# Transposed products with the activations' high and low parts side by side

## The chip, the cores and the metric

One NeuronCore of one Trainium2 chip runs the whole program. The metric is the device time of one execution in microseconds (us); lower is better. The engines are TensorE (PE in the profile, its loads of a stationary operand PEld), VectorE (DVE), ScalarE (ACT), GpSimd (POOL) and SyncE (SP), which issues the DMAs.

## The reference

One decoder block over 256 positions of width 1024, all in float32:

```python
h = rms_norm(x, norm1_g)
proj = h @ w_in                                  # [q | k | v | z | xBC | dt | gate_attn | gate_ssd]
y_attn = moba_attention(rms_norm(q), rms_norm(k), v) @ w_attn_o        # 16 heads of 64
y_ssd = ssd_mixer(z, xbc, dt_raw, ...) @ w_ssd_o                       # 2048 -> 1024
mixed = sigmoid(g_attn) * y_attn + sigmoid(g_ssd) * y_ssd
x = x + mixed @ w_out
x = x + peer_ffn(rms_norm(x, norm2_g), w_peer_q, keys1, keys2, u_tab, v_tab)

def peer_ffn(xn, w_q, keys1, keys2, u_tab, v_tab):
    q = (xt @ w_q).reshape(T, 8, 256)            # 8 heads
    s1 = einsum('thd,hkd->thk', q[..., :128], keys1)    # 128 keys each
    s2 = einsum('thd,hkd->thk', q[..., 128:], keys2)
    v1, i1 = top_k(s1, 16); v2, i2 = top_k(s2, 16)
    sv, pos = top_k(all sums v1 + v2, 16)        # 16 of 16384 experts for each head and token
    gw = softmax(sv)
    act = einsum('td,thkd->thk', xt, u_tab[eidx])
    return einsum('thk,thkd->td', gelu(act) * gw, v_tab[eidx])
```

## The kernel before

A product in float32 precision is made of three matmuls in TensorE's fp32r type. Each operand is held as a high part (the value rounded to fp32r) and a low part (the rest), and high by high, high by low and low by high are summed in PSUM. Weights come from HBM as 392 tiles of 128x1024 (512 KB), in one fixed order: the blocks of w_in, then w_attn_o and w_ssd_o, w_out, w_peer_q, the 128 tiles of u_tab, the 128 of v_tab. For each tile, `ahead` issues the load into a ring of three raw buffers, the copy on ScalarE that makes the high part (`wh`, line 128) and the subtraction that makes the low part (`wl`, on VectorE in line 138, on GpSimd in line 133 for one tile in three or four); `wh` and `wl` are rings of four. In this text the subtraction is called the split. `next_w` hands out the next tile and lets this pipeline run three tiles ahead.

The work goes through the weights in that order.

- The blocks of w_in: for each of 8 groups, products for q and k, v, z, and the two inputs of the convolution. The steps of attention, convolution and scan are generators in the list `active`; `tick()`, called twice in every product of 8 chunks, advances each by one step, so that their work falls between the matmuls. The last 8 blocks are the gates (line 695): 128 columns of each gate to a block.
- The output projections (line 705): for each of four blocks of 256 columns, `pA` (attention, 8 chunks) and `pS` (scan, 16 chunks), mixed with the gates into `mh` and `ml`.
- w_out with the residual, the second norm, and the transposed activations `xh`, `xl`.
- The queries, one product for each of 8 heads, with `head_scores` behind it. Here the top-16 searches and the one-hot selections begin (`picks`, paced so that each step is queued on VectorE behind the latest split).
- u_tab, 64 pairs of tiles (`u_pair`): every token against every expert, then Gelu into `gA`. When the picks are done (`start` is the pair at which that happens), the gate matrices follow, built from one-hots eight tokens at a time between the remaining pairs, and multiplied into `gA`.
- v_tab, 64 pairs of tiles, summed in four PSUM banks over all experts.

A *transposed* product (`product_T`, and the loop of `u_pair`) has the weights as the stationary operand and the activations as the moving one, 256 columns (the tokens) wide; its output has 128 weight columns on the partitions and the tokens along the free axis. Two such column tiles share a PSUM buffer of 512 columns. Three PSUM buffers (tag "mm") take turns for all products. A chunk is 128 rows of the summed dimension:

```python
mm(ps[:, ct], h[:, c], xh[:, k], start=k == 0, stop=False)
mm(ps[:, ct], h[:, c], xl[:, k], start=False, stop=False)
mm(ps[:, ct], lo[:, c], xh[:, k], start=False, stop=k == 8 * n - 1)
```

The order of instructions on each engine is made by the framework's scheduler from the order of the program, the dependencies and a few explicit ones (`issue_after`).

Of the kernel before, what the change touches and what calls it, by code (L numbers as in the profile page):

```python
# [9 lines left out]
F32 = mybir.dt.float32  # L10
F32R = mybir.dt.float32r
# [50 lines left out]
def tile_hybrid_block(ctx: ExitStack, tc: tile.TileContext, x, n1g, wblk, wdt, qkg, cw, cb, dtb,  # L62
# [11 lines left out]
    neghalf = const.tile([128, 16], F32, name="neghalf")  # L74
    V.memset(neghalf, -0.5)
    xt = const.tile([128, 2, D], F32, name="xt")
    hTh = const.tile([128, 8, T], F32R, name="hTh", tag="nh")
    hTl = const.tile([128, 8, T], F32R, name="hTl", tag="nl")

    def K(ins):  # L80

# [8 lines left out]
    def f32(ap):  # L90
        return ap.bitcast(F32)
# [50 lines left out]
    def next_w():  # L142
        i = state["next"]
        ahead()
        state["next"] += 1
        h, lo = parts.pop(i)
        return h, lo
# [3 lines left out]
    def tick():  # L151

        for it in list(active):
            if next(it, "end") == "end":
                active.remove(it)
# [9 lines left out]
    def product_T(ps, n, xh, xl):  # L165

        for ct in range(2):
            for f in range(n):
                h, lo = next_w()
                h = h.rearrange("p (c n) -> p c n", c=8)  # L170
                lo = lo.rearrange("p (c n) -> p c n", c=8)
                for c in range(8):
                    k = 8 * f + c
# [3 lines that stand above are left out]
                    if c % 4 == 3:  # L177
                        tick()

    def natural_w():  # L180
        w = []
        for f in range(2):
            h, lo = next_w()
            w += [(h[:, 256 * c:256 * c + 256], lo[:, 256 * c:256 * c + 256]) for c in range(4)]
        return w

    def product_half(ps, tt, w, xh, xl, late=False):
        s = slice(128 * tt, 128 * tt + 128)
        for f in range(2):
            terms = [(k, i) for k in range(4 * f, 4 * f + 4) for i in range(3)]  # L190
            if late:
                terms.sort(key=lambda t: (0, 2, 1)[t[1]])
            for n, (k, i) in enumerate(terms):
                lhs, rhs = ((xh, w[k][0]), (xh, w[k][1]), (xl, w[k][0]))[i]
                mm(ps[:, tt], lhs[:, k, s], rhs, start=f == n == 0, stop=f == 1 and n == 11)  # L195
            tick()

    def product_N(ps, xh, xl, late=False):

        w = natural_w()  # L200
        for tt in range(2):
            product_half(ps, tt, w, xh, xl, late)

    def rstd_of(pool, ss, n, inv, name):
        r = pool.tile([128, n], F32, name=name + "m", tag=f"rm{n}", bufs=2)
# [8 lines left out]
    def ps_tile(tag, name):  # L214
        return psum.tile([128, 512], F32, name=name, tag=tag, bufs={"mm": 3, "tr": 2, "at": 3}[tag])

    with tc.tile_pool(name="pa", bufs=1) as pa, ExitStack() as ctx2:
# [101 lines left out]
        dist = pa.tile([128, 384], F32, name="dist")  # L319
        mask = pa.tile([128, 384], F32, name="mask")  # L320

        attnh = pa.tile([128, 8, T], F32R, name="attnh")
        attnl = pa.tile([128, 8, T], F32R, name="attnl")
        yh = pa.tile([128, 16, T], F32R, name="yh")
        yl = pa.tile([128, 16, T], F32R, name="yl")


        dth = pa.tile([128, 2, 32], F32, name="dth")
# [8 lines left out]

        def w384(name):
            return wk.tile([128, 384], F32, name=name, tag="w384", bufs=W384)

        def half(t):
            return t.rearrange("p (a n) -> p a n", a=2)

        def decay():
            wdh = wk.tile([128, 8, 32], F32R, name="wdh", bufs=1)
# [320 lines left out]
            vsb[b] = v  # L666
            yield

        def take_gate(g, ps):
            A.activation(tg[:, :, g], ps, AF.Tanh, scale=0.5)  # L670
            yield

        active.append(decay())
# [17 lines left out]
            product_N(half(ps), hTh, hTl)  # L691
            active.append(zgate(g, ps))
        for g in range(NG):
            ps = half(ps_tile("mm", f"psg{g}"))
            product_T(ps, 1, hTh, hTl)
            active.append(take_gate(g, ps))
        while active:
            tick()

# [3 lines left out]
        mh = pm.tile([128, 8, T], F32R, name="mh", bufs=1)  # L703
        ml = pm.tile([128, 8, T], F32R, name="ml", bufs=1)
        for b in range(4):
            pA = ps_tile("mm", "pA").rearrange("p (c t) -> p c t", c=2)
            product_T(pA, 1, attnh, attnl)
            pS = ps_tile("mm", "pS").rearrange("p (c t) -> p c t", c=2)
            product_T(pS, 2, yh, yl)
            m1 = pm.tile([128, 2, T], F32, name="m1", tag="w512", bufs=W512)  # L710
            V.scalar_tensor_tensor(m1, tg[:, 0, 2 * b:2 * b + 2], 1.0, pA, op0=OP.add, op1=OP.mult)
            m2 = pm.tile([128, 2, T], F32, name="m2", tag="w512", bufs=W512)
            V.scalar_tensor_tensor(m2, tg[:, 1, 2 * b:2 * b + 2], 1.0, pS, op0=OP.add, op1=OP.mult)
            V.tensor_tensor(m1, m1, m2, op=OP.add)
            A.activation(mh[:, 2 * b:2 * b + 2], m1, AF.Copy, scale=0.5)
            V.scalar_tensor_tensor(ml[:, 2 * b:2 * b + 2], m1, 0.5, f32(mh[:, 2 * b:2 * b + 2]),
                                   op0=OP.mult, op1=OP.subtract)
        ss4 = pm.tile([128, 2, 4], F32, name="ss4", bufs=1)
        ss2 = pm.tile([128, 2], F32, name="ss2", bufs=1)
        xh = const.tile([128, 8, T], F32R, name="xh", tag="nh")  # L720
        xl = const.tile([128, 8, T], F32R, name="xl", tag="nl")

        def residual(b, tt, po):
            s = slice(256 * b, 256 * b + 256)
# [67 lines left out]
    def head_scores(h, ps):  # L792
        qT = tk.tile([128, 2, T], F32, name="pqT", tag="pqT")
        if h == 0:
            q = tk.tile([128, 2, T], F32, name="pq", tag="pqT")
            A.activation(q, ps, AF.Copy)
            yield
            ps = ps_tile("tr", "pqt").rearrange("p (c t) -> p c t", c=2)
            for f in range(2):
                for tt in range(2):  # L800
                    nc.tensor.transpose(ps[:, f, 128 * tt:128 * tt + 128], q[:, tt, 128 * f:128 * f + 128], ident)
            yield
        A.activation(qT, ps, AF.Copy)
        yield
        yield
        p2 = ps_tile("tr", "pss").rearrange("p (a n) -> p a n", a=4)
        for tt in range(2):
            for f in range(2):
                mm(p2[:, 2 * tt + f], qT[:, f, 128 * tt:128 * tt + 128], ks[:, f, h], start=True, stop=True)
        yield  # L810
        s = tk.tile([128, 4, 128], F32, name="sco", tag="sco", bufs=8)
        A.activation(s, p2, AF.Copy)
        scores[h] = s
# [103 lines left out]
    def halves(a, b):  # L917

        r = []
        for i in range(2):  # L920
            lo, hi = max(a, 64 * i), min(b, 64 * i + 64)
            if lo < hi:
                r.append((lo, hi, gA[i][:, lo - 64 * i:hi - 64 * i]))
        return r

    def u_pair(jp):
        ps = ps_tile("mm", "psu").rearrange("p (j t) -> p j t", j=2)
        for jj in range(2):
            h, lo = next_w()
            h = h.rearrange("p (c n) -> p c n", c=8)  # L930
            lo = lo.rearrange("p (c n) -> p c n", c=8)
            for c in range(8):
                mm(ps[:, jj], h[:, c], xh[:, c], start=c == 0, stop=False)  # L933
                mm(ps[:, jj], h[:, c], xl[:, c], start=False, stop=False)  # L934
                mm(ps[:, jj], lo[:, c], xh[:, c], start=False, stop=c == 7)  # L935
                if c % 4 == 3:
                    tick()
        td = done["t"]
        (_, _, dst), = halves(2 * jp, 2 * jp + 2)
        if td < T:  # L940
            A.activation(dst[:, :, td:], ps[:, :, td:], AF.Gelu)
        if td > 0:
            gt = pb.tile([128, 2, T], F32, name="gel", tag="gel", bufs=2)
            A.activation(gt[:, :, :td], ps[:, :, :td], AF.Gelu)
            V.tensor_tensor(dst[:, :, :td], dst[:, :, :td], gt[:, :, :td], op=OP.mult)
# [34 lines left out]
    active.append(picks)  # L980
    active.insert(0, head_scores(0, psq0))
    for h in range(1, 8):
        ps = ps_tile("mm", "psq").rearrange("p (c t) -> p c t", c=2)
        product_T(ps, 1, xh, xl)
        active.insert(0, head_scores(h, ps))
    start = None
    for jp in range(64):
        u_pair(jp)
        if start is None and (done["picks"] == 2 or jp >= 30):
            while done["picks"] < 2:  # L990
                tick()
            tkctx.close()
            pb2 = ctx.enter_context(tc.tile_pool(name="pb2", bufs=1))
            gA[1] = pb2.tile([128, 64, T], F32, name="gA1")
            start = jp
            one_hots(0)
        elif start is not None:
            n = 62 - start
            k = jp - start - 1
            if k < n:  # L1000
                for q in range(32 * k // n, 32 * (k + 1) // n):
                    gate_group(q, 2 * jp + 2)
                    if q + 1 < 32:
                        one_hots(q + 1)
# [96 lines left out]
```

## Time and profile before

| | |
|---|---|
| median of 3 runs | 1246.58 us (1246.37 to 1247.64) |
| the profiled execution | 1246.86 us, of it 1244.8 us in the span of the profile |
| TensorE busy | 1228.4 us, 9005 matmuls |
| VectorE busy | 897.4 us |
| ScalarE busy | 633.9 us |
| GpSimd busy | 296.0 us |
| granted TensorE clock, mean | 0.997 of full |
| gates / output projections / queries | 282 to 342 / 342 to 411 / 444 to 491 us |
| u_tab before the gate matrices, with them / v_tab | 491 to 654, 654 to 892 / 892 to 1244 us |

Matmuls are pipelined: one is shown as busy from its start to its modelled end, and the next one starts before that, so the pace of a stretch is read from start to start. In a view of windows the columns are the stretch, its length, the busy time of PE, PEld, DVE, ACT and POOL with the count of instructions, the granted clock, the DMA share and GB/s. In a timeline they are start and duration in us, engine, line, operation, what is written and read, and in brackets how long the engine had stood idle before and what it waited for. In a group of instructions, the busy time in us and the mean of one in ns stand behind the bar.

### The profile page before, as it was taken

Reading aid. Unit: us, or ns where it says so; the run is one execution under the profiler, and the core shown is the slowest. Engines: PE = TensorE matmul, PEld = TensorE weight load, DVE = VectorE, ACT = ScalarE, POOL = GpSimd, SP = SyncE. Lnnn points to the kernel's source line nnn. Section 1 sums busy time; section 2 is a strip of 40 time slices with the busy share of each in tenths; the row PEclk is TensorE's granted clock in tenths of the full one; section 3 lists DMA queues with packets and bytes.
Section 4 is the critical chain, followed back from the end, with each engine's and each line's share of the span. In section 5 each row is a group of like instructions: output and inputs, shape, how many; then the busy total and the mean of one; then the engine's idle time right before and its main releaser. Section 6 shows DMA issues by size and latency. Waiting matters only on the chain.

```text
span 1244.8 us, 22716 instructions
## 1 busy us (share of the span) xinstructions
PE 1228.4 (99%) x9005; PEld 1140.7 (92%) x9005; DVE 897.4 (72%) x1583; ACT 633.9 (51%) x975; POOL 296.0 (24%) x160
## 2 busy tenths in 40 slices
PE   8999999999999999999999999999999999999998
PEld 6989989999999999999999999999988888888887
DVE  6888989899334566688697888999855555555554
ACT  5666666666434454554544544444445454444442
POOL 3355354444222122232323222222100000000000
PEclk8999999999999999999999999999999999999999
DMA  5434444444455464546555455444455555555553
GB/s 193 173 136 154 169 156 166 153 145 143 171 202 186 137 220 153 185 155 209 180 172 168 153 170 160 157 168 158 165 195 194 195 188 201 188 194 194 196 193 118
DMA packets 60345, 215.15 MB, mean 173 GB/s; under 512 B 7600, under 2 KB 8144, under 8 KB 60112
## 3 DMA queue, kind: packets, MB, share of 16 engines
q1 hardware_dynamic: 60240, 213.71, 50.3%
q8 instruction: 70, 1.15, 0.4%
q14 instruction: 35, 0.29, 0.1%
HBM read 212.60 MB, written 1.08 MB: 172 GB/s over the span
## 4 chain that ended last, share of the span: by engine, by line
PE 90%; DVE 6%; POOL 2%; issue 0%; DMA 0%; SPq 0%; ACT 0%; DVEq 0%; POOLq 0%
PE psu L933 10%; PE psu L935 10%; PE psu L934 10%; PE py L1020 9%; PE py L1022 9%; PE py L1021 9%; PE psqk L195 3%; PE psg L971 2%; PE psv L195 2%; PE psz L195 2%; PE pO L195 2%; POOL p L483 1%; DVE acc L538 1%; PE pS L175 1%; PE pS L176 1%; PE pS L174 1%
## 5 line engine op out<-in xcount | busy, mean ns | idle before, releaser
L128 ACT ACTIVATE wh<-wr 128x1024 fp32r<-128x1024 f32 x392 | 413.7, 1056 | 348.8 <-PE psu L934 96.2
L138 DVE TENSOR_TENSOR wl<-wr,wh 128x1024 fp32r<-128x1024 f32 x312 | 384.9, 1235 | 201.8 <-ACT wh L128 200.7
L133 POOL TENSOR_TENSOR wl<-wr,wh 128x1024 fp32r<-128x1024 f32 x79 | 204.0, 2583 | 421.4 <-ACT wh L128 355.3
L933 PE MATMUL psu<-xh,wh 128*128 128x256 f32 x1024 | 292.5, 286 | 0.0
L935 PE MATMUL psu<-xh,wl 128*128 128x256 f32 x1024 | 289.7, 283 | 0.0
L934 PE MATMUL psu<-xl,wh 128*128 128x256 f32 x1024 | 289.7, 283 | 0.0
L1020 PE MATMUL py<-wh,hh 128*128 128x512 f32 x512 | 199.2, 389 | 0.0
L1021 PE MATMUL py<-wl,hh 128*128 128x512 f32 x512 | 199.2, 389 | 0.0
L1022 PE MATMUL py<-wh,hl 128*128 128x512 f32 x512 | 199.2, 389 | 0.0
L934 PEld LDWEIGHTS psu<-xl,wh 128*128 128x128 f32 x1024 | 196.5, 192 | 0.0
L935 PEld LDWEIGHTS psu<-xh,wl 128*128 128x128 f32 x1024 | 196.3, 192 | 0.2 <-DVE wl L138 0.2
L933 PEld LDWEIGHTS psu<-xh,wh 128*128 128x128 f32 x1024 | 196.2, 192 | 0.0
L1022 PEld LDWEIGHTS py<-wh,hl 128*128 128x128 f32 x512 | 96.1, 188 | 20.1
L1021 PEld LDWEIGHTS py<-wl,hh 128*128 128x128 f32 x512 | 96.1, 188 | 19.9
L1020 PEld LDWEIGHTS py<-wh,hh 128*128 128x128 f32 x512 | 96.1, 188 | 19.8
L1012 ACT ACTIVATE hh<-gA 128x512 fp32r<-128x512 f32 x64 | 40.4, 632 | 88.8 <-PE py L1021 88.7
L1013 DVE SCALAR_TENSOR_TENSOR hl<-gA,hh 128x512 fp32r<-128x512 f32 x64 | 44.4, 693 | 52.3 <-ACT hh L1012 52.3
L958 DVE TENSOR_TENSOR og<-oh,g 128x1024 f16<-128x1024 f16 x64 | 58.5, 952 | 1.0
L538 DVE SCALAR_TENSOR_TENSOR acc<-u,cws,acc 128x254 f32<-128x254 f32 (+2 forms) x96 | 51.2, 566 | 0.5 <-ACT acc L534 0.4
L976 ACT ACTIVATE gA<-psg 128x24 f32<-128x24 f32 (+28 forms) x70 | 18.6, 281 | 64.4 <-DVE gA L974 55.2
L483 POOL TENSOR_SCALAR p<-p,rs 128x128 f32<-128x128 f32 (+1 forms) x32 | 41.1, 1298 | 38.5 <-DVE rs L481 38.5
L974 DVE TENSOR_TENSOR gA<-gA,psg 128x256 f32<-128x256 f32 (+12 forms) x120 | 38.1, 352 | 10.2 <-PE psg L971 9.8
(320 smaller groups left out, 2411.4 us busy)
## 6 DMA issues: line engine op xcount, KB each, us to landing
wr<-in_u_tab SPq DMA_DIRECT2D x128, 512.0 KB, 3.3
wr<-in_v_tab SPq DMA_DIRECT2D x128, 512.0 KB, 3.2
wr<-in_wblk SPq DMA_DIRECT2D x88, 512.0 KB, 3.3
wr<-in_wso SPq DMA_DIRECT2D x16, 512.0 KB, 4.1
wr<-in_wpq SPq DMA_DIRECT2D x16, 512.0 KB, 4.1
ar<-acT SPq DMA_DIRECT2D x8, 512.0 KB, 3.9
wr<-in_wao SPq DMA_DIRECT2D x8, 512.0 KB, 3.3
wr<-in_wou SPq DMA_DIRECT2D x8, 512.0 KB, 3.9
```

The source lines that it names most:

```text
L128: K(A.activation(h, r, AF.Copy))
L133: state["pool"] = nc.gpsimd.tensor_tensor(lo, r, f32(h), op=OP.subtract)
L138: state["wl"] = K(V.tensor_tensor(lo, r, f32(h), op=OP.subtract))
L195: mm(ps[:, tt], lhs[:, k, s], rhs, start=f == n == 0, stop=f == 1 and n == 11)
L538: V.scalar_tensor_tensor(acc[:, i, sh:], u[:, i, :T - sh], cws[:, ct, 3 - sh:4 - sh], acc[:, i, sh:], op0=OP.mult, op1=OP.add)
L933: mm(ps[:, jj], h[:, c], xh[:, c], start=c == 0, stop=False)
L934: mm(ps[:, jj], h[:, c], xl[:, c], start=False, stop=False)
L935: mm(ps[:, jj], lo[:, c], xh[:, c], start=False, stop=c == 7)
L958: V.tensor_tensor(og[:, i], oh[:, 1], g2[:, i, t].rearrange("p (g e) -> p g e", e=2)[:, :, None, :] .to_broadcast([128, 4, 128, 2]), op=OP ...
L1020: mm(o, hh[:, jj, s], h[:, c], start=j == 0, stop=False)
L1021: mm(o, hh[:, jj, s], lo[:, c], start=False, stop=False)
L1022: mm(o, hl[:, jj, s], h[:, c], start=False, stop=j == 127)
```

## The change

The high and the low part of the transposed activations now lie side by side in one tile (`hT`, `attn`, `yy`, `xx`: 2 x 256 columns for each chunk). A new function `wide` makes a transposed product of one column tile with two matmuls per chunk: the weights' high part against both parts at once, 512 columns into the two halves of a PSUM buffer, and the weights' low part against the high part, 256 columns added to the second half. The halves are summed afterwards: ScalarE copies the second half to SBUF, VectorE adds the first. It is used for the gates, the output projections, the queries (from the second head on) and the pairs of u_tab before `start`; the convolution's inputs and the later pairs of u_tab keep the three matmuls.

```diff
-    hTh = const.tile([128, 8, T], F32R, name="hTh", tag="nh")
-    hTl = const.tile([128, 8, T], F32R, name="hTl", tag="nl")
+    hT = const.tile([128, 8, 2, T], F32R, name="hT", tag="nx")
+    hTh, hTl = hT[:, :, 0], hT[:, :, 1]
...
+    def wide(ps, n, x):
+
+        for f in range(n):
+            h, lo = next_w()
+            h = h.rearrange("p (c n) -> p c n", c=8)
+            lo = lo.rearrange("p (c n) -> p c n", c=8)
+            for c in range(8):
+                k = 8 * f + c
+                last = k == 8 * n - 1
+                pair = [(ps, h[:, c], x[:, k]), (ps[:, 1], lo[:, c], x[:, k, 0])]
+                for i, (o, a, b) in enumerate(reversed(pair) if last else pair):
+                    mm(o, a, b, start=k == i == 0, stop=last and i == 1)
+                if c % 4 == 3:
+                    tick()
...
-        def take_gate(g, ps):
-            A.activation(tg[:, :, g], ps, AF.Tanh, scale=0.5)
+        def take_gate(g, i, ps):
+            s = wk.tile([128, T], F32, name="gs", tag="sqy")
+            A.activation(s, ps[:, 1], AF.Copy)
+            V.tensor_tensor(s, s, ps[:, 0], op=OP.add)
+            A.activation(tg[:, i, g], s, AF.Tanh, scale=0.5)
             yield
...
         for g in range(NG):
-            ps = half(ps_tile("mm", f"psg{g}"))
-            product_T(ps, 1, hTh, hTl)
-            active.append(take_gate(g, ps))
+            for i in range(2):
+                ps = half(ps_tile("mm", f"psg{g}"))
+                wide(ps, 1, hT)
+                active.append(take_gate(g, i, ps))
...
         for b in range(4):
-            pA = ps_tile("mm", "pA").rearrange("p (c t) -> p c t", c=2)
-            product_T(pA, 1, attnh, attnl)
-            pS = ps_tile("mm", "pS").rearrange("p (c t) -> p c t", c=2)
-            product_T(pS, 2, yh, yl)
-            m1 = pm.tile([128, 2, T], F32, name="m1", tag="w512", bufs=W512)
-            V.scalar_tensor_tensor(m1, tg[:, 0, 2 * b:2 * b + 2], 1.0, pA, op0=OP.add, op1=OP.mult)
-            m2 = pm.tile([128, 2, T], F32, name="m2", tag="w512", bufs=W512)
-            V.scalar_tensor_tensor(m2, tg[:, 1, 2 * b:2 * b + 2], 1.0, pS, op0=OP.add, op1=OP.mult)
-            V.tensor_tensor(m1, m1, m2, op=OP.add)
-            A.activation(mh[:, 2 * b:2 * b + 2], m1, AF.Copy, scale=0.5)
-            V.scalar_tensor_tensor(ml[:, 2 * b:2 * b + 2], m1, 0.5, f32(mh[:, 2 * b:2 * b + 2]),
-                                   op0=OP.mult, op1=OP.subtract)
+            m = [pm.tile([128, 2, T], F32, name=f"m{i}", tag="w512", bufs=W512) for i in range(2)]
+            for i, (n, x) in enumerate(((1, attn), (2, yy))):
+                for c in range(2):
+                    ps = half(ps_tile("mm", ("pA", "pS")[i]))
+                    wide(ps, n, x)
+                    s = pm.tile([128, T], F32, name="ms", tag="ms", bufs=4)
+                    A.activation(s, ps[:, 1], AF.Copy)
+                    V.tensor_tensor(s, s, ps[:, 0], op=OP.add)
+                    k = 2 * b + c
+                    V.scalar_tensor_tensor(m[i][:, c], tg[:, i, k], 1.0, s, op0=OP.add, op1=OP.mult)
+                    if i == 1:
+                        o = m[0][:, c]
+                        V.tensor_tensor(o, o, m[1][:, c], op=OP.add)
+                        A.activation(mh[:, k], o, AF.Copy, scale=0.5)
+                        V.scalar_tensor_tensor(ml[:, k], o, 0.5, f32(mh[:, k]), op0=OP.mult, op1=OP.subtract)
...
-        A.activation(qT, ps, AF.Copy)
+            A.activation(qT, ps, AF.Copy)
+        else:
+            for f in range(2):
+                A.activation(qT[:, f], ps[f][:, 1], AF.Copy)
+            yield
+            for f in range(2):
+                V.tensor_tensor(qT[:, f], qT[:, f], ps[f][:, 0], op=OP.add)
         yield
         yield
...
+    def u_wide(jp):
+
+        (_, _, dst), = halves(2 * jp, 2 * jp + 2)
+        for jj in range(2):
+            ps = half(ps_tile("mm", "psu"))
+            wide(ps, 1, xx)
+            A.activation(dst[:, jj], ps[:, 1], AF.Copy)
+            V.tensor_tensor(dst[:, jj], dst[:, jj], ps[:, 0], op=OP.add)
+        A.activation(dst, dst, AF.Gelu)
...
-        ps = ps_tile("mm", "psq").rearrange("p (c t) -> p c t", c=2)
-        product_T(ps, 1, xh, xl)
+        ps = []
+        for f in range(2):
+            ps.append(half(ps_tile("mm", "psq")))
+            wide(ps[f], 1, xx)
         active.insert(0, head_scores(h, ps))
     start = None
     for jp in range(64):
-        u_pair(jp)
+        (u_wide if start is None else u_pair)(jp)
         if start is None and (done["picks"] == 2 or jp >= 30):
```

The tiles `attnh` and `attnl` become the halves of `attn`, `yh` and `yl` those of `yy`, `xh` and `xl` those of `xx`; what else reads or writes them is as before.

## Rows read from the trace of the kernel before

**Rows 1.** page: busy us by engine; shares of the chain that ended last

```profile
PE 1228.4 (99%) x9005; PEld 1140.7 (92%) x9005; DVE 897.4 (72%) x1583; ACT 633.9 (51%) x975; POOL 296.0 (24%) x160
...
PE 90%; DVE 6%; POOL 2%; issue 0%; DMA 0%; SPq 0%; ACT 0%; DVEq 0%; POOLq 0%
```

**Rows 2.** windows of the four changed stages

```profile
282.00:342.00 60.00, 59.87 (x498) 57.65 (x497) 36.55 (x59) 32.29 (x55) 20.83 (x13) 1.00 0.46 159
342.00:411.00 69.00, 69.00 (x578) 69.00 (x577) 28.21 (x30) 27.74 (x29) 19.10 (x8) 1.00 0.56 189
...
444.00:491.00 47.00, 47.00 (x399) 47.00 (x398) 29.59 (x111) 23.02 (x29) 11.98 (x5) 1.00 0.55 187
491.00:654.00 163.00, 163.00 (x1361) 162.85 (x1360) 128.96 (x397) 81.01 (x94) 48.60 (x19) 1.00 0.53 179
```

**Rows 3.** timeline of TensorE from 560 us: first and last of 19

```profile
559.73 0.28 PE L935 MATMUL psu<-xh,wl 128*128 128x256 f32 x1
...
561.89 0.28 PE L935 MATMUL psu<-xh,wl 128*128 128x256 f32 x1
```

**Rows 4.** timeline of TensorE from 1000 us: first and last of 55

```profile
999.73 0.39 PE L1022 MATMUL py<-wh,hl 128*128 128x512 f32 x1
...
1011.97 0.39 PE L1022 MATMUL py<-wh,hl 128*128 128x512 f32 x1
```

**Rows 5.** groups of TensorE by line and form

```profile
L174 PE MATMUL psg<-hTh,wh 128*128 128x256 f32 x128 | 36.9, 288 | 0.0
...
L174 PE MATMUL pS<-yh,wh 128*128 128x256 f32 x128 | 35.9, 280 | 0.0
...
L174 PE MATMUL psq<-xh,wh 128*128 128x256 f32 x112 | 32.3, 289 | 0.0
```

**Rows 6.** tile psu: duration in ns, first and last start

```profile
L933 PE MATMUL psu<-xh,wh x1024: 281/283/364, 491.0 to 892.1; 128*128 128x256 f32 x171
```

**Rows 7.** the chain that ended last, in order of time: start, us

```profile
659.90 0.94 PE psg L971 x16
```

**Rows 8.** groups by line and form on VectorE and ScalarE

```profile
L725 DVE TENSOR_TENSOR xt<-xt,pO 128x256 f32<-128x256 f32 x8 | 3.1, 416 | 4.0 <-PE pO L195 4.0
...
L524 ACT ACTIVATE attnh<-po 128x256 fp32r<-128x256 f32 x8 | 3.0, 374 | 0.9 <-PE po L521 0.9
```

**Rows 9.** windows of 5.8 us: one of the gates, three of the table

```profile
293.50:299.30 5.80, 5.67 (x45) 5.05 (x45) 5.77 (x10) 4.65 (x7) 2.62 (x3) 1.00 0.59 201
...
543.20:549.00 5.80, 5.80 (x51) 5.80 (x50) 5.76 (x10) 2.60 (x3) 1.16 (x1) 1.00 0.51 181
...
607.20:613.00 5.80, 5.80 (x50) 5.80 (x50) 3.06 (x18) 2.60 (x3) 2.40 (x1) 1.00 0.44 145
...
630.50:636.30 5.80, 5.80 (x51) 5.80 (x50) 5.73 (x8) 2.60 (x3) 1.74 (x1) 1.00 0.52 184
```

**Rows 10.** timeline of VectorE in the table stage

```profile
533.39 1.23 DVE L138 TENSOR_TENSOR wl<-wr,wh 128x1024 fp32r<-128x1024 f32 x1 [2.70 <-ACT wh L128]
...
556.99 2.96 DVE L138 TENSOR_TENSOR wl<-wr,wh 128x1024 fp32r<-128x1024 f32 x1
...
565.86 1.21 DVE L138 TENSOR_TENSOR wl<-wr,wh 128x1024 fp32r<-128x1024 f32 x1
...
620.12 1.22 DVE L138 TENSOR_TENSOR wl<-wr,wh 128x1024 fp32r<-128x1024 f32 x1 [0.28 <-ACT wh L128]
...
638.13 1.21 DVE L138 TENSOR_TENSOR wl<-wr,wh 128x1024 fp32r<-128x1024 f32 x1
```

**Rows 11.** timeline of ScalarE, table stage

```profile
532.30 1.06 ACT L128 ACTIVATE wh<-wr 128x1024 fp32r<-128x1024 f32 x1 [1.69 <-PE psu L934]
...
563.39 1.06 ACT L128 ACTIVATE wh<-wr 128x1024 fp32r<-128x1024 f32 x1 [3.40 <-DMA wr<-in_u_tab]
...
619.02 1.06 ACT L128 ACTIVATE wh<-wr 128x1024 fp32r<-128x1024 f32 x1 [0.25 <-issue]
```

**Rows 12.** waits, 491 to 654 us: total us, times, longest us

```profile
PEld psu L935 <- DVE wl L138: 0.2, 1, 0.2
```

More of the change, by code (lines that the diff above doesn't have):

```diff
@@ L202, in product_N, with half @@
             product_half(ps, tt, w, xh, xl, late)
+    def half(t):
+        return t.rearrange("p (a n) -> p a n", a=2)
     def rstd_of(pool, ss, n, inv, name):
@@ L320, in tile_hybrid_block @@
         mask = pa.tile([128, 384], F32, name="mask")
[L322 to L325, printed above, removed]
+        attn = pa.tile([128, 8, 2, T], F32R, name="attn")
+        attnh, attnl = attn[:, :, 0], attn[:, :, 1]
+        yy = pa.tile([128, 16, 2, T], F32R, name="yy")
+        yh, yl = yy[:, :, 0], yy[:, :, 1]
         dth = pa.tile([128, 2, 32], F32, name="dth")
@@ L339, in w384 @@
             return wk.tile([128, 384], F32, name=name, tag="w384", bufs=W384)
-        def half(t):
-            return t.rearrange("p (a n) -> p a n", a=2)
         def decay():
@@ L705, in tile_hybrid_block @@
         for b in range(4):
-            pA = ps_tile("mm", "pA").rearrange("p (c t) -> p c t", c=2)
-            product_T(pA, 1, attnh, attnl)
-            pS = ps_tile("mm", "pS").rearrange("p (c t) -> p c t", c=2)
-            product_T(pS, 2, yh, yl)
-            m1 = pm.tile([128, 2, T], F32, name="m1", tag="w512", bufs=W512)
-            V.scalar_tensor_tensor(m1, tg[:, 0, 2 * b:2 * b + 2], 1.0, pA, op0=OP.add, op1=OP.mult)
-            m2 = pm.tile([128, 2, T], F32, name="m2", tag="w512", bufs=W512)
-            V.scalar_tensor_tensor(m2, tg[:, 1, 2 * b:2 * b + 2], 1.0, pS, op0=OP.add, op1=OP.mult)
-            V.tensor_tensor(m1, m1, m2, op=OP.add)
-            A.activation(mh[:, 2 * b:2 * b + 2], m1, AF.Copy, scale=0.5)
-            V.scalar_tensor_tensor(ml[:, 2 * b:2 * b + 2], m1, 0.5, f32(mh[:, 2 * b:2 * b + 2]),
-                                   op0=OP.mult, op1=OP.subtract)
+            m = [pm.tile([128, 2, T], F32, name=f"m{i}", tag="w512", bufs=W512) for i in range(2)]
[13 more added lines that the diff above has]
+                        V.scalar_tensor_tensor(ml[:, k], o, 0.5, f32(mh[:, k]), op0=OP.mult, op1=OP.subtract)
         ss4 = pm.tile([128, 2, 4], F32, name="ss4", bufs=1)
         ss2 = pm.tile([128, 2], F32, name="ss2", bufs=1)
-        xh = const.tile([128, 8, T], F32R, name="xh", tag="nh")
-        xl = const.tile([128, 8, T], F32R, name="xl", tag="nl")
+        xx = const.tile([128, 8, 2, T], F32R, name="xx", tag="nx")
+        xh, xl = xx[:, :, 0], xx[:, :, 1]
         def residual(b, tt, po):
```

## Prediction

> **What bounds the kernel now.** I read the page first: TensorE is busy 99% of the span, and the chain that ended last is 90% TensorE [rows 1]. The busy time by stages comes next: in the four stages that the change touches TensorE stands still for 0.13 us in all, and its granted clock is 1.00 in each, the upper of its two levels (2.4 GHz); VectorE has room in the output projections (28 of 69 us), less with the queries (30 of 47) and little in the table stage up to 654 us (129 of 163) [rows 2]. So a product gets shorter only if its matmuls leave TensorE faster, and what that may cost is read from VectorE's queue.
>
> Pace is read from start to start, not from the durations, which overlap: 256-wide matmuls leave every 2.16 / 18 = 0.1200 us [rows 3], 512-wide ones of the same type every 12.24 / 54 = 0.2267 us [rows 4]. Twice the columns cost 1.89 times as much, so some 0.013 us per matmul doesn't depend on the width.
>
> **What the change takes off TensorE.** A chunk of 128 rows of a transposed product costs three 256-wide matmuls, 0.360 us. Afterwards it is one 512-wide (weights' high part against both parts of the activations) and one 256-wide: 0.2267 + 0.1200 = 0.3467 us, 0.0133 us less. No row alternates the widths. I take the sum of the two paces, since each already holds the load of a new 128x128 operand; if a load that follows a narrow matmul were not hidden, the chunk could save nothing (lower bound 0), and if the fixed part fell away in one of the two, 0.027 us. Both paces come from stretches without waits, with a load before each matmul, so I hold either end for unlikely; they lie, by the count below, 11.5 us to either side.
>
> Chunks, counted as matmuls of high by high part [rows 5]: gates 128, output projections 128 for the longer of the two and half as many for the shorter, queries 112. For the table: only pairs before the gate matrices are changed. TensorE starts the table at 491.0 us [rows 6] and the first gate group at 659.9 us [rows 7]; (659.9 - 491.0) / 5.76 is 29 pairs and a rest. In the code the first group falls two pairs after the pair that opens the gate matrices (32 groups over 62 - start pairs, the first slot rounds to none), so start = 26 and pairs 0 to 26 are changed: 27 x 16 = 432 chunks. The number of ticks per product stays (two per eight chunks), and the head's extra step falls a tick before its scores are asked for, so start stays. Sum: 864 x 0.0133 = 11.5 us.
>
> **What it adds.** A 128-column tile now fills a whole PSUM buffer in two halves, and each of 16 + 16 + 14 + 54 = 100 tiles needs a copy on ScalarE and an add on VectorE. The nearest rows: 0.374 us for the copy (128x256 out of PSUM), 0.416 us for the add with one PSUM operand [rows 8]. Gate tanh, Gelu and the mixing keep their element counts, in smaller or SBUF-fed pieces. ScalarE gets 37 us in stages where it is about half busy or less [rows 2]: nothing. VectorE gets 42 us:
>
> - Gates: 16 adds, 6.7 us, in a stage with 36.6 of 60 us busy. VectorE is full up to 300 us [rows 9], and the last heads' products (the py matmuls) wait for it; I take 0, bounded by 1.2 us (three adds) above and, as nothing there waits for gates, 0 below.
> - Output projections: 41 us idle for 6.7 us of adds and some smaller mixing pieces: 0. The tail before w_out is now copy, add, multiply, add, split on half tiles instead of the same on whole ones; before, TensorE is busy to the stage's last moment [rows 2], and w_out's first products use k-chunks mixed earlier, which cover the tail. Without that cover some 2.5 us would be open (six steps of about 0.42 us); I take 0.
> - Queries: 5.8 us into 17 us of idle time: 0.
> - Table: 54 adds, 22.4 us, into 34 us of idle time. Not all of it is where the adds fall.
>
> **Where the table stage gives time back.** VectorE's windows [rows 9] swing between some 3 us in 5.8 and full, as top-16 steps and one-hot selections pile up and single operations are stretched (one split took 2.96 us, another 1.23 [rows 10]). A product can't start its low matmuls before its wl split, and the split sits in VectorE's queue with the picks and, now, the adds. The reserve is read in two stretches; tile numbers count table loads from 0.
>
> *First.* The split of tile 17 starts at 533.39 us after an idle 2.70 us; its ScalarE half began at 532.30 [rows 10, 11], when tile 14 started on TensorE and so tile 13 had freed its buffer (ring of four). From there VectorE has no gap until tile 24's split ends at 556.99 + 2.96 = 559.95 us [rows 10]. TensorE needs that at 532.30 + 10 x 2.88 = 561.1 us: reserve 1.15 us. Afterwards ten tiles take 10 x 2.773, 1.07 us less, and eight adds (products 14 to 21) come ahead of the split, 3.33 us. Late by 3.33 + 1.07 - 1.15 = 3.2 us.
>
> *Second.* Tile 47's split starts at 620.12 us, its ScalarE half at 619.02; VectorE is nearly gapless to the end of tile 51's split at 639.34 us [rows 10, 11]. TensorE needs it at 619.02 + 7 x 2.88 = 639.2: no reserve, and the only wait of a weight load for a split between 491 and 654 us (0.2 us) fits it [rows 12]. Afterwards 0.75 us from the faster tiles and six adds, 2.50 us: 3.3 us.
>
> Between the two, windows like 3.06 us in 5.8 [rows 9] let the queue recover, so I add nothing there. TensorE gives back 3.2 + 3.3 = 6.5 us. Bounds: 0, if the new order puts picks behind splits; upwards below.
>
> Loads on SP's queue are neither added nor moved; each still follows the split that frees its buffer. The add also waits in VectorE's queue for its product and copy, with the next split and picks behind it, and ScalarE's Gelu waits for the add, with later weight copies behind it. A PSUM buffer is now refilled three tiles later instead of three pairs: an add may be 2 x 2.77 = 5.5 us late, less its copy and itself 4.7 us. The split's own reserve, 1.15 us and none, runs out first.
>
> The Trainium skill speaks against the change: TensorEngine Tiling (Array Packing), section PSUM Bottleneck, says that a faster TensorE leaves PSUM's evacuation as the possible bottleneck, to be shared by both engines. By evacuation alone (0.37 + 0.42 us a tile) it would take nothing off the 11.5 us; the trace agrees with the warning through the queue only.
>
> **The sum.** The profiled execution took 1246.86 us (span 1244.8 and 2.1 around it), 0.28 us above the median shown. 1246.86 - 11.5 + 6.5 = 1241.9; against the median 1241.6. I predict 1241.7 us. 0.2% (2.5 us) is about what a measurement can tell from no change.
>
> **The rivals.**
>
> - *All of the saving stays*: 1235.3 us. For it: 34 us of idle VectorE time against 22.4 us of adds, and an order of instructions made anew. Against it: reserves of 1.15 and 0 us.
> - *The table stage eats the saving*: ten of the 28 windows between 491 and 654 us have VectorE busy 5.59 us or more in 5.8 (two stand in [rows 9]). If none has reserve, each loses 0.83 us of adds and 0.21 us of pace: 10.4 us, 1246 us.
> - *Slower.* A late split frees its raw buffer late: tile 24's split ended 559.95, the load landed 3.44 us after, and the next weight copy on ScalarE waited for it [rows 10, 11]. Now a PSUM copy stands behind that weight copy, its add on VectorE behind that, and the next split behind the add. The round of three tiles is 3.44 + 1.06 + 1.23 = 5.7 us of 8.3, so it carries on once VectorE's queue adds more than 2.6 us (before: 1.4 us, split at 565.86 after a copy ended 564.45; three adds make 2.65). With two further stretched operations in each stretch (2.96 - 1.23 = 1.7 us): 10.4 + 4 x 1.7 = 17.2 us, 1252 us; it is slower from 14 us given back.
> - *The wide matmul costs no more than a narrow one*: 864 x 0.12 = 104 us off, 1143 us. Against it stand the 0.2267 us of [rows 4], in a stretch without waits: 1 in 100. The Trainium skill (TensorE: Matmul & The Clock Gate, section Back-to-back issue gap) gives about 131 ns for a sustained 512-column matmul, an estimate of 94 us off here by that page; the trace disagrees.
>
> **How the numbers follow.** All of the saving 0.25; forecast (4 to 9 us given back) 0.35; eaten up (9 to 14 us) 0.19; slower 0.20; wide matmul cheap 0.01. Faster 0.61, same 0.19, slower 0.20. The range reaches from the full saving with a little rate to spare, 1234.5, to 15.4 us given back, 1250.5. Where the sign is open, the likeliest case's own range is 1239 to 1244.
>
> **What would show it.** In the changed kernel's profile: a 512-wide and a 256-wide matmul every 0.347 us together in gates, projections, queries and early table; 100 copies near 0.37 us and 100 adds near 0.42 us; gates, projections and queries shorter by 1.7, 2.6 and 1.5 us; TensorE idle on wl splits, 3 us at the first selections and 3 us at the second. Idle time on the PSUM adds instead would make the reserve argument wrong; a chunk off 0.347 us the rate; a start other than 26 the count.

## The result, and the profile after

The changed kernel takes 1241.11 us (median of 6 runs, 1239.3 to 1241.75) against 1246.63 us for the kernel before (median of 6 runs beside it): a ratio of 0.995, 95% interval 0.994 to 0.9961. 1241.7 was predicted. The time is right within a measurement's error, but two terms of the sum behind it are not: a chunk saves less than forecast, and the table stage gives back almost nothing.

The page of the changed kernel, busy us by engine and shares of the chain that ended last:

```profile
PE 1220.7 (99%) x8141; PEld 1093.9 (88%) x8141; DVE 940.0 (76%) x1699; ACT 659.8 (53%) x1080; POOL 295.3 (24%) x160
...
PE 88%; DVE 7%; POOL 2%; ACT 1%; issue 1%; DMA 0%; SPq 0%; DVEq 0%; POOLq 0%
```

Against [rows 1] TensorE has 864 matmuls and 7.7 busy us fewer, VectorE 42.6 busy us more (42 were costed); TensorE still sets the end. Windows of the four changed stages (columns: us, then PE, PEld, DVE, ACT, POOL):

```profile
288.30:339.70 51.40, 51.18 (x301) 42.96 (x300) 34.80 (x57) 33.14 (x67) 17.77 (x11) 1.00 0.47 156
339.70:407.00 67.30, 67.30 (x385) 58.65 (x384) 44.39 (x61) 33.16 (x48) 19.87 (x8) 1.00 0.59 195
440.50:486.10 45.60, 45.60 (x285) 40.67 (x284) 32.54 (x121) 23.03 (x37) 12.00 (x5) 1.00 0.57 191
486.10:640.70 154.60, 154.07 (x881) 134.06 (x880) 138.68 (x445) 93.31 (x143) 49.02 (x18) 1.00 0.54 181
```

From the first matmul of a stage to the first of the next, the trace of before has 51.72, 69.12 and 46.95 us for gates, projections and queries, that of after 51.32, 67.34 and 45.68. The gains are 0.4, 1.8 and 1.3 us; 1.7, 2.6 and 1.5 were expected. For the table I take the stretch from its first matmul to the first gate group in the chain: 659.9 - 491.0 = 168.9 us before [rows 6, 7] and 652.4 - 486.1 = 166.3 us after, 2.6 us less, where the prediction had some 0.75 us more.

The pace is read from the chain in order of time (start, us, engine, tile, line, matmuls):

```profile
315.89 23.93 PE psg L192 x136
...
345.48 11.21 PE pS L192 x64
...
492.85 57.74 PE psu L192 x328
...
550.91 57.83 PE psu L192 x328
```

Two matmuls are a chunk: 57.74 / 164 = 0.352 us in the table, 23.93 / 68 = 0.352 in the gates, 11.21 / 32 = 0.350 in the projections. The forecast was 0.3467. The queries, whose products have other work between them, come nearest: 5.57 / 16 = 0.348 for the two products of a head (first row, from the chain), and about 0.346 inside a product (two narrow matmuls five chunks apart in the timeline, 1.73 / 5):

```profile
454.09 5.57 PE psq L192 x32
```

```profile
454.16 0.28 PE L192 MATMUL psq<-xx,wl 128*128 128x256 f32 x1
...
455.89 0.28 PE L192 MATMUL psq<-xx,wl 128*128 128x256 f32 x1
```

TensorE's waits between 486.1 and 640.7 us (us in total, times, longest), and the new copies and adds (ns at least, median, at most; first and last start):

```profile
PEld psu L192 <- DVE gA L962: 0.8, 1, 0.8
PE psu L192 <- DVE gA L962: 0.5, 1, 0.5
```

```profile
L961 ACT ACTIVATE gA<-psu x54: 362/383/388, 489.2 to 641.2; 128x256 f32<-128x256 f32 x54
L962 DVE TENSOR_TENSOR gA<-gA,psu x54: 396/408/425, 490.1 to 645.6; 128x256 f32<-128x256 f32 x54
```

No wait on a split is left, where 6.5 us were forecast; the one wait of its matmuls is for an add, half a microsecond. How close the splits came is read from the end of a split and the start of the first matmul that uses its low part. The first two rows are tile 24's split and that matmul; the last row is that matmul of tile 51, whose split ran from 627.62 to 628.83 us:

```profile
551.82 1.20 DVE L139 TENSOR_TENSOR wl<-wr,wh 128x1024 fp32r<-128x1024 f32 x1
555.22 0.28 PE L192 MATMUL psu<-xx,wl 128*128 128x256 f32 x1
...
631.36 0.28 PE L192 MATMUL psu<-xx,wl 128*128 128x256 f32 x1
```

The splits of tiles 24 and 51, forecast to be 3.2 and 3.3 us late, were 2.2 and 2.5 us early; the least reserve of any split in the changed pairs is 1.5 us (tile 23).

### The profile page after: what moved, and what is told of

Its sections match the earlier page's. It is cut to its first block, busy times and chain, and to the rows that moved or that the text cites. A ratio compares the mean times of both kernels' runs of the same rounds, so it can differ in the third digit from the quotient of the medians.

```text
span 1237.3 us, 21233 instructions
## 1 busy us (share of the span) xinstructions
PE 1220.7 (99%) x8141; PEld 1093.9 (88%) x8141; DVE 940.0 (76%) x1699; ACT 659.8 (53%) x1080; POOL 295.3 (24%) x160
## 4 chain that ended last, share of the span: by engine, by line
PE 88%; DVE 7%; POOL 2%; ACT 1%; issue 1%; DMA 0%; SPq 0%; DVEq 0%; POOLq 0%
PE psu L192 10%; PE py L1061 9%; PE py L1062 9%; PE py L1063 9%; PE psu L972 6%; PE psu L973 6%; PE psu L974 6%; PE pS L192 4%; PE psg L192 3%; PE psq L192 3%; PE psqk L211 3%; PE psg L1010 2%; PE psv L211 2%; PE pA L192 2%; PE psz L211 2%; PE pO L211 2%
## 5 line engine op out<-in xcount | busy, mean ns | idle before, releaser
L972 PE MATMUL psu<-xx,wh 128*128 128x256 f32 x592 | 170.2, 287 | 0.0
L973 PE MATMUL psu<-xx,wh 128*128 128x256 f32 x592 | 167.5, 283 | 0.0
L974 PE MATMUL psu<-xx,wl 128*128 128x256 f32 x592 | 167.4, 283 | 0.0
L192 PE MATMUL psu<-xx,wh 128*128 128x512 f32 x432 | 149.3, 399 | 0.5 <-DVE gA L962 0.5
L973 PEld LDWEIGHTS psu<-xx,wh 128*128 128x128 f32 x592 | 113.5, 192 | 0.0
L974 PEld LDWEIGHTS psu<-xx,wl 128*128 128x128 f32 x592 | 113.3, 191 | 0.0
L972 PEld LDWEIGHTS psu<-xx,wh 128*128 128x128 f32 x592 | 113.3, 191 | 0.0
L192 PE MATMUL psu<-xx,wl 128*128 128x256 f32 x432 | 112.5, 281 | 0.0
L192 PEld LDWEIGHTS psu<-xx,wh 128*128 128x128 f32 x432 | 77.8, 188 | 15.5 <-DVE gA L962 0.8
L192 PEld LDWEIGHTS psu<-xx,wl 128*128 128x128 f32 x432 | 81.6, 189 | 4.9
```

The lines of the kernel that those rows point to most:

```text
L192: mm(o, a, b, start=k == i == 0, stop=last and i == 1)
```

## The experiments

**Order of the two widths.** Two orders keep the work and change how often TensorE alternates.

Grouped, in `wide`:

```python
jobs = [(0, c) for c in range(7 if end else 8)] + [(1, c) for c in range(8)]
if end: jobs.append((0, 7))
for j, (i, c) in enumerate(jobs):      # i == 0: the wide matmul, i == 1: the narrow one
```

> In a weight tile all 8 wide matmuls come first and the 8 narrow ones behind them (in the last tile of a product the last wide one closes the bank, behind the narrow ones); nothing else differs from the changed kernel. Theory 1, the switch between widths costs: after the change the table's pairs take 0.352 us per wide and narrow matmul, where the v-table stage has 0.2266 us for a 512-column matmul between its like and 0.120 us for a 256-column one; then most pairs here take 0.3467 us, the table stage loses 432 x 0.0057 = 2.5 us, the gates about 0.7 and the projections 0.7, and the time is about 1237 us. Theory 2, a wide matmul whose moving operand is the activations costs 0.235 us whatever stands beside it: then the wide ones keep 0.235 us, the narrow ones take 0.120 us, a pair 0.353 to 0.355, and the time stays at 1240 to 1243 us.

1239.23 us (ratio to before 0.9932, 0.9916 to 0.9949). The timeline (the first two rows are the starts of two weight tiles, 8 chunks each, in one product of the projections; the last three are one product of the table and the start of the next):

```profile
362.15 2.02 PE L194 MATMUL pS<-yy,wh 128*128 128x512 f32 x8
...
364.98 1.33 PE L194 MATMUL pS<-yy,wh 128*128 128x512 f32 x5
```

```profile
570.17 2.00 PE L194 MATMUL psu<-xx,wh 128*128 128x512 f32 x8
572.01 1.12 PE L196 MATMUL psu<-xx,wl 128*128 128x256 f32 x8
572.96 2.00 PE L194 MATMUL psu<-xx,wh 128*128 128x512 f32 x8
```

2.79 / 8 = 0.349 us for a chunk of the table, between the theories and nearer theory 1; in the projections 2.83 / 8 = 0.354, worse than the 0.350 of the plain alternation.

Zigzag:

```diff
-                for i, (o, a, b) in enumerate(reversed(pair) if last else pair):
+                for i, (o, a, b) in enumerate(reversed(pair) if c % 2 else pair):
```

> Every second chunk has its narrow matmul ahead of the wide one, so that the widths change once per chunk and not twice. Theory 1 (each change of width costs): half of the extra 0.0057 us per chunk goes, 1.2 us of the table stage and some 2 us in all, about 1239 us. Theory 2 (the wide one itself costs 0.235 us): no change, 1240 to 1242 us.

1239.26 us (0.994, 0.9923 to 0.9956). From its chain:

```profile
346.89 11.20 PE pS L192 x64
...
494.04 57.15 PE psu L192 x328
```

57.15 / 164 = 0.3485 us in the table, 0.350 in the projections. So the order matters in the table, though not per change of width: a product of 16 matmuls has 14 changes in the kernel as changed, 8 here and 2 when grouped, and the surplus over 0.3467 us is 5.4, 1.8 and 2 ns a chunk. In the queries this order gained nothing (5.59 us for 16 chunks against 5.57).

**All matmuls wide.** This settles whether a 512-column matmul over the activations is slower by itself.

```diff
-                pair = [(ps, h[:, c], x[:, k]), (ps[:, 1], lo[:, c], x[:, k, 0])]
+                pair = [(ps, h[:, c], x[:, k]), (ps, lo[:, c], x[:, k])]
```

> The narrow matmul of each chunk is made as wide as the other: the low weights times both halves, into the whole bank, so that all 16 matmuls of a product have 512 columns and the activations as moving operand (the product gets the low times low term too; VectorE and ScalarE do the same). Theory 2, a wide matmul over the activations costs about 0.235 us by itself: a product of 16 takes 3.73 to 3.76 us, a chunk 0.470. Theory 3, a wide one costs 0.2267 us as in the v-table stage and what was added came from mixing the widths: a product takes 3.63 us, a chunk 0.4533. Either way the time is some 85 to 105 us longer, about 1330 to 1345 us.

1330.22 us (one run). Its chain:

```profile
361.18 14.94 PE pS L192 x64
...
542.38 74.37 PE psu L192 x328
```

74.37 / 328 = 0.2267 us in the table: theory 3 there. The paces of [rows 3, 4] hold for each width among its like, and in the table the two together take more than their sum. Whether the change of width does it, or something that goes with it (the narrow matmul adds into one half of the PSUM buffer, the wide one into both), no run separates. But the projections have 14.94 / 64 = 0.2334 us, with no narrow matmul near: there a wide one is slower by itself. So is it in the grouped order, where the narrow ones keep 0.96 / 8 = 0.120 us (chain of that run):

```profile
362.31 1.86 PE pS L194 x8
364.18 0.96 PE pS L196 x8
```

The sum of the two paces is thus 0.2334 + 0.1200 = 0.3534 us in the projections, and there the plain alternation, at 0.350, takes less than the sum.

**The place of the operand.** In the projections the activations lie 32 bytes past a multiple of 64 in their partitions, elsewhere on one. An unused tile shifts them, first with all matmuls wide, then with the zigzag:

```diff
+        pa.tile([128, 8], F32, name="shift")
         attn = pa.tile([128, 8, 2, T], F32R, name="attn")
```

> The run with 512 columns in all matmuls, with an unused tile of 32 bytes per partition ahead of attn and yy, which moves both from 32 bytes past a multiple of 64 onto one; the activations of gates, queries and table lie on a multiple of 64 already. That run had 3627 ns for 16 matmuls in gates, queries and table (226.7 each) and 3731 to 3732 ns in the projections (233.2 each). Theory D, the place of the moving operand makes the difference: the projections come to 3627 ns too, and their stage is 24 x 0.104 = 2.5 us shorter, 1327.5 us. Theory E, it is the stage (what other engines do there): still 3731 ns and 1330 us.

> Every second chunk with its narrow matmul first, and attn and yy moved by the same 32 bytes. By theory D the projections' products go from 2800 ns to the 2787 that this order had in gates and table: 24 x 0.013 = 0.3 us less than the 1239.3 us of that order alone, 1238 to 1240 us. By theory E no change, 1239.3 us.

All wide: 1329.91 us (one run), and the projections as before, 14.93 / 64 = 0.2333 us: theory D falls for that stream.

```profile
360.68 14.93 PE pS L192 x64
...
542.05 74.36 PE psu L192 x328
```

With the zigzag the same shift took the projections from 0.350 to 11.15 / 32 = 0.3484 us, the table's pace, as D had it:

```profile
345.95 11.15 PE pS L192 x64
...
492.99 57.15 PE psu L192 x328
```

The time was 1238.71 us (0.9938, 0.9925 to 0.9952), the lowest of all versions that leave nothing out, 2.4 us below the kernel as changed; that is about the 0.2% that can be told, and the chain's pieces say the same (57.15 against 57.74 us in the table, 11.15 against 11.21 in the projections). So 32 bytes can matter in the mixed stream, and they are not the reason for the 0.2333 us; what that is stays open.

**The table's part alone.** The table's pairs as before the change:

```diff
-        (u_wide if start is None else u_pair)(jp)
+        u_pair(jp)
```

> Gates, projections and queries stay changed; the table's pairs are all done as before the change (three narrow matmuls per chunk, no copy, no add). If each stage's gain stands by itself, the time lies about 3 us above the changed kernel: 1243 to 1244.5 us, of which the windows give gates 0.4, projections 1.8 and queries 1.4 us of gain. If the table's part gives nothing (its copies and adds eat the 432 x 0.008 us), it equals the changed kernel, 1240 to 1241.5 us.

1243.47 us (0.9977, 0.9968 to 0.9987), 2.3 us above the changed kernel: the table's gain stands by itself, with adds and all.

**VectorE's load.** Three runs change its work in the wide pairs. Without copy and add:

```diff
-            A.activation(dst[:, jj], ps[:, 1], AF.Copy)
-            V.tensor_tensor(dst[:, jj], dst[:, jj], ps[:, 0], op=OP.add)
-        A.activation(dst, dst, AF.Gelu)
+            A.activation(dst[:, jj], ps[:, 0], AF.Gelu)
```

> The wide pairs of the table leave out the copy of the second half and the add on VectorE, so these pairs lack the products with the low parts; Gelu reads the first half from PSUM, once per product. VectorE loses 52 adds of about 0.41 us, 21 us of its 138.7 busy us in the table's wide stage. If TensorE alone sets that stage (the copy and the add cost nothing there), it stays at 154.6 us within 0.7 and the time at 1239 to 1241.5 us. If VectorE's late splits still cost something in it, the stage is 2 to 6 us shorter, 1235 to 1238 us.

1250.0 us (1.0026, 1.0016 to 1.0036): with 21 us less work on VectorE the kernel is 9 us slower, which neither theory had. The timeline of GpSimd, and TensorE's waits:

```profile
620.90 2.54 POOL L134 TENSOR_TENSOR wl<-wr,wh 128x1024 fp32r<-128x1024 f32 x1 [6.07 <-ACT wh L129]
629.36 13.21 POOL L134 TENSOR_TENSOR wl<-wr,wh 128x1024 fp32r<-128x1024 f32 x1 [5.92 <-ACT wh L129]
```

```profile
PE psu L192 <- POOL wl L134: 6.1, 1, 6.1
...
PE psu L192 <- DVE wl L139: 1.3, 1, 1.3
```

One GpSimd split took 13.21 us instead of 2.5. Windows around it (PE, PEld, DVE, ACT, POOL, granted clock):

```profile
634.00:637.00 3.00, 2.55 (x15) 1.88 (x13) 3.00 (x7) 1.42 (x2) 3.00 (x1) 1.00 0.23 90
637.00:640.00 3.00, 0.00 (x0) 0.00 (x0) 3.00 (x4) 0.00 (x0) 3.00 (x1) 0.79 0.00 0
640.00:643.00 3.00, 0.37 (x1) 0.38 (x2) 0.37 (x1) 0.00 (x0) 2.57 (x1) 0.50 0.00 0
643.00:646.00 3.00, 3.00 (x12) 2.56 (x12) 0.00 (x0) 0.00 (x0) 0.00 (x0) 0.57 0.79 274
```

VectorE runs full until 640.37 us, all its operations in that row reading SBUF alone; GpSimd ends 2.2 us after the row, about what a free split takes. TensorE's clock then stands at the lower of its two levels, and its next products run at half pace until about 646 us. In the kernel as changed, the same GpSimd split got in, by its times, at an add that reads PSUM; VectorE's timeline there:

```profile
627.62 1.21 DVE L139 TENSOR_TENSOR wl<-wr,wh 128x1024 fp32r<-128x1024 f32 x1
628.75 1.21 DVE L915 TENSOR_TENSOR eq<-eq,xf 128x2048 f16<-128x2048 f16 x1
629.89 0.41 DVE L962 TENSOR_TENSOR gA<-gA,psu 128x256 f32<-128x256 f32 x1
630.22 2.55 DVE L919 TENSOR_TENSOR eq<-eq 128x1024 f16<-128x1024 f16 x1
```

GpSimd's split ran there from 627.97 to 632.22 us: held up to the add, it took its 2.3 us from there, while the next VectorE operation waited (2.55 us for one that takes 0.68). The Trainium skill (SBUF — State Buffer, section Who interferes with whom) says that a VectorE instruction with two SBUF inputs contends with a GpSimd one that reads SBUF, and, where it speaks of VectorE's two-port modes, that whoever issues first has the shared ports for the whole instruction. The trace agrees with the first (13.21 against 2.5 us); here GpSimd didn't get in between the instructions of an unbroken row either.

The test of that reading gives five of GpSimd's splits to VectorE (the low parts are left out here too):

```diff
-... and not 116 <= i < 124 and i % (3 if i >= 88 else 4) == PS[i >= 88]):
+... and not 116 <= i < 124 and not n_u + 42 <= i < n_u + 58 and i % (3 if i >= 88 else 4) == PS[i >= 88]):
```

> Like the run without copy and add in the table's wide pairs (their products with the low parts are left out), but five of GpSimd's splits, among the table's tiles 42 to 57, are given to VectorE. That run lost 9 us where one GpSimd split took 13.21 us, beside an unbroken row of VectorE operations with two inputs in SBUF. Theory A, VectorE's row kept GpSimd from memory: no such split is left there, the stall of 6.5 us and the slow clock behind it go, 1239.5 to 1242 us. Theory B, the late weight came from the loads or from the lack of the adds otherwise: TensorE still waits there, 1247 to 1251 us.

1241.37 us (0.9957, 0.994 to 0.9974): theory A. TensorE's only wait in the stage is the small one, 1.3 us, for the split of tile 21, as in the run without copy and add. Without the copies and adds, and with five more splits on VectorE, the time is that of the changed kernel: the copies and adds cost next to nothing there in the end. That wait stands where the changed kernel has none, so the order of VectorE's queue counts beside its load.

```profile
PE psu L192 <- DVE wl L139: 1.3, 1, 1.3
```

More work on VectorE, a second add for each product, then for every second one:

```diff
             V.tensor_tensor(dst[:, jj], dst[:, jj], ps[:, 0], op=OP.add)
+            V.tensor_tensor(dst[:, jj], dst[:, jj], ps[:, 0], op=OP.add)
```

> Each product of the table's wide pairs gets a second add of the same half on VectorE (its gate input is then another number). VectorE gets 52 x 0.41 = 21 us more in a stage of 154.6 us in which it is busy for 138.7. If its idle time can be used in full, the stage becomes VectorE's, 160 to 162 us, and the time about 1247 us. If its splits come late one by one before that, as the prediction had it, the stage grows by more, 10 to 21 us, to 1251 to 1262 us. If VectorE had slack enough, no change.

> Only every second product of the table's wide pairs gets the second add of the same half (its gate input is then another number): 27 x 0.41 = 11 us more on VectorE, half of the run that added 21.6 us and lost 7.4. If VectorE's late stretches lose from the first add on, about half of that: 1244.5 to 1246 us. If there is slack for about 11 us more before the splits come late, 1240.5 to 1242 us. If the loss is a matter of which operations meet GpSimd's splits, anything between 1241 and 1249 us.

1248.7 us with all (1.0011, 1.0001 to 1.002), 1244.3 us with half (0.9983, 0.9973 to 0.9992): 7.5 and 3.1 us above the changed kernel. TensorE's waits in the wide stage, with all and with half:

```profile
PEld psu L192 <- DVE wl L139: 4.2, 3, 2.5
PE psu L192 <- DVE wl L139: 3.0, 2, 2.1
PE psu L192 <- ACT gA L961: 1.3, 1, 1.3
PE psu L192 <- DVE gA L963: 0.4, 1, 0.4
```

```profile
PE psu L192 <- DVE wl L139: 1.8, 1, 1.8
...
PE psu L192 <- DVE gA L964: 0.5, 1, 0.5
```

The larger ones are waits on VectorE's splits: with all adds for tile 21 (its matmul starts at 550.83 us) and tile 51 (639.89 us), with half for tile 21 alone (550.25 us). Tile 51 is the one that the prediction had named, tile 21 lies in its first stretch, three tiles ahead of the one named. With all adds TensorE also waited 1.7 us near 549 and 545 us for a copy of a PSUM half and for an add, a kind of wait that the prediction had put behind the splits. Behind the waits the granted clock is near the lower level (0.62 and 0.58 in two windows of the run with all adds, TensorE busy throughout), and the half pace adds to the loss:

```profile
551.00:554.00 3.00, 3.00 (x12) 2.63 (x13) 3.00 (x18) 1.22 (x2) 0.00 (x0) 0.62 0.49 175
640.00:643.00 3.00, 3.00 (x12) 2.57 (x13) 3.00 (x9) 1.42 (x2) 0.00 (x0) 0.58 0.85 294
```

**The changed kernel again.**

> The changed kernel once more, unaltered, on the same chip as the others. By the runs so far 1239 to 1241.8 us, with a chunk of the table at 0.3525 us; its first part (up to the gates) shows whether the 1.5 us by which the first profile was shorter there come again (288.3 us) or were that execution's (289.3 us, the mean of the first four experiments' being 289.5).

1241.27 us (0.9951, 0.9935 to 0.9968), the table's chunk again at 57.74 / 164. The matmuls of the gates (first and last start) in the first profile and in this one:

```profile
L192 PE MATMUL psg<-hT,wh x128: 387/397/505, 288.3 to 339.4; 128*128 128x512 f32 x128
```

```profile
L192 PE MATMUL psg<-hT,wh x128: 387/397/504, 290.6 to 341.7; 128*128 128x512 f32 x128
```

Before the change the first start was 289.8 us. The 1.5 us that the first profile seemed to gain ahead of the gates were that execution's.

## Why the time was right, and which steps were not

- *The chunk* (11.5 us): mis-sized. The mechanism held, and both single paces were right in the table (0.2267 us in the run with all wide, 0.1200 in [rows 3]); what failed was "I take the sum of the two paces". Alternating, they take 0.350 to 0.352 us, in the queries 0.348, so a chunk saves 0.008 to 0.012 us: by pace some 1.0 us in the gates, 1.9 in the projections, 3.4 in the table and 1.3 in the queries, 7.6 us together. In the table changing the order won back up to 3.6 ns a chunk, so it is the sequence and not the wide matmul by itself; what in the sequence costs is not shown. In the projections it is the other way: the wide one has a surplus of its own (0.2334 us) that stays unexplained, and alternating hides part of it.
- *The table gives back 6.5 us*: wrong; it gives back 0.5, and that for an add on PSUM, which by the prediction's own sign ("Idle time on the PSUM adds instead") speaks against the reserve argument. The places were nearly right: with more adds TensorE waits in the two stretches named. The lateness was wrong, because VectorE's order was carried over from before. There the split of tile 24 took 2.96 us and stood behind a gapless row [rows 10]; afterwards no VectorE split of the stage took more than 1.60 us (rows of VectorE's splits, below), as the operations stretched in the two stretches were picks. From the start of tile 17's split to the end of tile 24's VectorE took 26.6 us before and 25.0 after, with seven adds in the row. In the second stretch a one-hot of the gate matrices stood ahead of tile 51's split before (633.64 us) and behind it after (632.70 us). The prediction had named this as its lower bound, "if the new order puts picks behind splits".

```profile
L139 DVE TENSOR_TENSOR wl<-wr,wh x35: 1199/1218/1598, 486.9 to 637.0; 128x1024 fp32r<-128x1024 f32 x35
```

- *The reserve*: the first dose of 54 adds cost about 0.5 us of waits, half a dose more 3.1 us of time, a full one more 7.5. With 1.5 us of reserve at its closest split the kernel as changed stands near the edge that the prediction put it over.
- *Gates, projections, queries: nothing given back.* No wait of TensorE for the new copies and adds was found there. The gates' stage gained 0.4 us of the 1.0 that the pace gives. Start to start, the gates' own matmuls take 0.9 us less, but the 16 scan matmuls among them (`py`) take 2.0 us in place of 1.6; weight loads of theirs now wait 0.3 us for an `m` from GpSimd and 0.2 us for one from VectorE.
- *The count* (start 26, 432 chunks, 100 copies and adds at 0.37 to 0.42 us): right; the page has 432 wide matmuls in the table, the rows above have 383 and 408 ns for the table's 54 copies and adds, and the other 46 have medians of 0.38 to 0.385 and 0.41 to 0.42 us.
- The sum comes out as 0.4 + 1.8 + 1.3 + 2.6 = 6.1 us by stages, against 5.5 us between the medians; single executions differ by some 2 us in the unchanged first part. With the two terms as measured the prediction's sum is 1246.86 - 7.6 + 0.5 = 1239.8 us, beside 1239.3 us for the profiled execution and 1241.1 for the median. An error of 3.9 us in the rate and one of 6 us in what is given back went opposite ways, so the predicted time was right partly by luck.

## What to carry to other kernels

Read the pace of a mixed stream from a mixed stream: two widths, each measured among its like, added up to less than they take side by side in the table and to more in the projections, and here a change in their order was worth a third of what the rewrite gained (1.9 of 5.5 us). A reserve read from one engine's queue belongs to that order of instructions; when the order is made anew, take the place of a stall from it, not the size. Before taking work off VectorE, see whether that work is what gives GpSimd an opening.

## What the runs showed that was not expected

- Removing 52 adds (21 us) from VectorE cost 9 us, because GpSimd's split took 13.21 us beside an unbroken row of SBUF-only VectorE operations.
- In the table, alternating 512 and 256 columns took 0.352 us a pair where the two alone take 0.3467; two of each in turn took 0.3485. In the projections alternating took 0.350 where the two alone take 0.3534.
- 512-column matmuls took 0.2267 us in the table and 0.2333 in the projections, in one kernel, with or without a shift of 32 bytes; the cause stays open.
- Behind the waits for splits near 640 us (without the adds) and near 551 and 640 us (with a second add) TensorE's granted clock read 0.50 to 0.62 in windows of 3 us. Where TensorE was busy throughout, such a window holds 12 matmuls, against 19 in the changed kernel at the full clock (551 to 554 us), so that a stall cost more than its own length.
